# Order of the two products in a block of fp32 matrix products: neighbours in opposite orders, or long and short alternating

## The chip, the core and the metric

The kernel runs on one core of one Trainium2 chip. The metric is the device time of one execution in microseconds (us); of the kernel before, the median of three runs is 771.32 us (771.22 to 771.48). A second kind of number comes from one further execution that was profiled instruction by instruction. Its engines are named as the profile names them: PE is the matrix engine, PEld its loading of stationary weights, DVE the vector engine, ACT the activation engine, POOL the general one, SP the one that issues most of the transfers.

## What is computed

Two decoder layers on 256 tokens of width 1024, all in float32 at the interface. The first mixes tokens with a short gated convolution, the second with dilated attention (8 heads, 3 dilation groups). Each is followed by a squared-ReLU MLP (1024 to 4096 to 1024) and a gated embedding, and a norm ends it all:

```python
h = x
for i in range(DEPTH):                      # DEPTH = 2
    hn = rmsnorm(h, norm_mix[i])
    if kind == 0:
        mixed = short_conv_mixer(hn, sc_w_in[j], sc_w_conv[j], sc_w_out[j])
    elif kind == 1:
        mixed = dilated_attention_mixer(hn, positions, attn_w_qkv[j], attn_w_o[j])
...
    h = h + mixed
    h = h + squared_relu_mlp(rmsnorm(h, norm_mlp[i]), mlp_w_up[i], mlp_w_down[i])
    ple_gate = jax.nn.sigmoid(rmsnorm(h, norm_ple[i]) @ ple_w_gate[i])
    h = h + ple_gate * (p[i].astype(h.dtype) @ ple_w_proj[i])
return rmsnorm(h, norm_final)
```

Almost all of the work is in the matrix products with the weights: every weight is read once from memory and used for 256 tokens.

## The kernel before

**A product in parts.** To keep float32 accuracy on the faster reduced format, each weight tile and each activation tile is held as a sum of two numbers, a high part (`whi`, `x[0]`) and a low part (`wlo`, `x[1]`). A product is then three: high by high, high by low, low by high. The function `block` (L379 to L411) issues them for one weight tile of 128 by 128, and there are three kinds of block.

- Kind "w" (wide): the weight is stationary. The two activation parts lie side by side in memory (`x[2]`), so that one matmul with `whi` and 512 columns makes two of the three products, into the two halves of a PSUM bank, and one matmul with `wlo` and 256 columns makes the third, into the bank's first half. The halves are added later by `sums` (L419). This is the kind of the up and down projections of the MLP, of queries and keys, and of most of the convolution's input, the output projections too. Below, the 256-column product is called the short one and the 512-column product the long one.
- Kind "n" (narrow): the weight is stationary too, but all three products have 256 columns.
- Kind "t" (turned): the activation is stationary and the weight streams, 384 columns for values ("v"), 512 or 256 in the last stage.

**The order of the work.** A plan written out by hand (`make_plan`, with `mlp_plan`, `gate_plan`, `last_plan`) lists blocks and, between them, steps such as evacuations of a bank (`up_out`, `down_out`, `qk_out`), statistics (`stat`, `spread`) and the attention's scores. The last loop of `tile_trunk` walks through it in order. Wide blocks come in pairs: for each row tile k of the weights one block for half 0 and one for half 1 (`for i in (0, 1)`), each half with a bank of its own (the name of the accumulator ends in i).

**The order within a wide block.** The line that the change replaces (L396) turns the two products of a block round when it belongs to half 1:

```python
products = ((dst[:, 0, :], wlo, x[0][:, k % 2, :]), (flat(dst), whi, flat(x[2][:, k % 2, :, :])))
...
products = products[::-1] if half and (key != "qkv" or col[1] or not col[2]) else products
```

So along a run of wide blocks the matmuls are short, long, long, short, short, long, long, short and so on. The exception is the bracket: the queries and keys of dilation group 0 (`col[1]` is the group) of every head but the first (`col[2]` is the head). There no block is turned round and the matmuls are short, long, short, long. These 16 blocks of a head stand right behind the values ("v") of the head before. The matmuls themselves are issued at L404, whatever their kind.

**Attention.** For each head from 1 to 7 the plan has the wide blocks of group 0 (16 blocks), then `scores` of the head before (from head 2 on; it issues matmuls of the values step at L736 and L746 and of the scores at L692 and L700), then groups 1 and 2 (32 blocks), with `turn` and its transposes (L726), then the values of the head (16 blocks of kind "t").

**The weights' way.** The weights come in slabs of up to 8 tiles (`load_to`, a transfer of up to 512 KB); ACT copies a slab to its high part (L368) and DVE subtracts it for the low part (L307, a helper). `weights` (L372) asks for slabs up to 5 ahead of the one in use, and there are 6 buffers for the split slabs and 5 for the raw ones.

Of the kernel before, what the change touches and what calls it, by code (L numbers as in the profile page):

```python
# [18 lines left out]
NK = D // P  # L19
NP = NK // 2  # L20
FF = 4 * D
# [210 lines left out]
def width(key):  # L232
    return {"v": GROUPS, "gate1": 4, "proj1": 4}.get(key, 1)
# [32 lines left out]
def tile_trunk(ctx: ExitStack, tc: tile.TileContext, plan, slabs, ap, out):  # L266
# [17 lines left out]
    def pair(name, tag="pair", dtype=F32R):  # L284

        if tag == "pair":
            t = apool.tile([P, 2, 2, S], dtype, tag=tag, bufs=PAIR_BUFS, name=name)
        else:
            t = cpool.tile([P, 2, 2, S], dtype, tag=tag, bufs=1, name=name)
        return t[:, :, 0, :], t[:, :, 1, :], t  # L290

    def bank(name):
        return psum.tile([P, 2, S], F32, tag="ps", name=name)
# [9 lines left out]
    def flat(t):  # L303
        return t.rearrange("p i s -> p (i s)")
# [16 lines left out]
    for op in plan:  # L321
        if op[0] != "do":
            key = ((*op[4], op[5]), 0) if op[0] == "w" else (op[4], op[5] if op[0] == "n" else 0)
            left[key] = left.get(key, 0) + 1
    rstd, rows, cur, mask, by_token = {}, {}, {}, {}, {}

    def gain(n, k):
        return gains[:, n * NK + k : n * NK + k + 1]
# [2 lines left out]
    offsets, n = [], 0  # L331
# [40 lines left out]
    def weights(item):  # L372
        si, at = place[item]
        split_to(si + min(LOOK, 1 + si // 3))
        hi, lo = parts[si]
        n = width(item[0]) * P
        return hi[:, at : at + n], lo[:, at : at + n]

    def block(kind, key, k, col, name, half, operand, m=0, cuts=1):  # L379
        name = (*name, half) if kind == "w" else name  # L380
        if name not in opened:
            acc[name] = bank("acc_" + "_".join(map(str, name)))
        left[name, half if kind == "n" else 0] -= 1
        whi, wlo = weights((key, k, col))
        x = state[operand][k // 2]
        if kind == "n":
            dst = acc[name][:, half, :]
            products = ((dst, wlo, x[0][:, k % 2, :]), (dst, whi, x[1][:, k % 2, :]), (dst, whi, x[0][:, k % 2, :]))

            products = (products[2], products[0], products[1]) if key == "proj0" else products  # L390
        elif kind == "w":

            dst = acc[name]
            products = ((dst[:, 0, :], wlo, x[0][:, k % 2, :]), (flat(dst), whi, flat(x[2][:, k % 2, :, :])))

            products = products[::-1] if half and (key != "qkv" or col[1] or not col[2]) else products  # L396
        else:
            n = width(key) * P // cuts
            whi, wlo = (t[:, m * n : (m + 1) * n] for t in (whi, wlo))
            dst = flat(acc[name])[:, :n]  # L400
            xhi, xlo = (t[:, k % 2, half * P : (half + 1) * P] for t in x[:2])
            products = ((dst, xhi, whi), (dst, xhi, wlo), (dst, xlo, whi))
        for n, (to, a, b) in enumerate(products):
            nc.tensor.matmul(  # L404
                to,
                a,
                b,
                start=n == 0 and name not in opened,
                stop=n == len(products) - 1 and left[name, half if kind == "n" else 0] == 0,
                skip_group_check=True,  # L410
            )  # L411
            opened.add(name)
# [269 lines left out]

    def scores(head):

        weights = cur["pr", head] = pair(f"sm{head}", dtype=F32)[2]
        ps = [psum.tile([P, 512], F32, tag="ps", name=f"sc{head}_{b}") for b in (0, 1)]
        rest = values(head - 1) if head else None
        for b in (0, 1):
            own = slice(b * P, (b + 1) * P)
            hi, lo, _ = state["qk"][head]  # L690
            for n, (q, k) in enumerate(((hi, hi), (hi, lo), (lo, hi))):
                nc.tensor.matmul(ps[b][:, :S], q[:, 0, own], k[:, 1, :], start=n == 0, stop=n == 2)  # L692
        if rest:
            rest()
        for b in (0, 1):
            for g in (1, 2):
                t = cur["qk", head, g]
                for r in (0, 1):
                    of, at = slice(b * P + r * 64, b * P + (r + 1) * 64), S + (g - 1 ^ r) * 64
                    nc.tensor.matmul(  # L700
                        ps[b][r * 64 : (r + 1) * 64, at : at + 64], t[:, 0, of], t[:, 1, of], start=True, stop=True
                    )
        for b in (0, 1):
            sm, p = flat(weights[:, b])[:, : S + P], ps[b][:, : S + P]
            stats = [spool.tile([P, 1], F32, tag=f"st{n}_{b}", name=f"st{n}_{head}_{b}") for n in range(2)]

            nc.vector.tensor_tensor_reduce(
                out=sm, in0=p, in1=mask[b], op0=ALU.add, op1=ALU.min, scale=-SCALE, scalar=-NEG, accum_out=stats[0]
            )
            nc.scalar.activation(sm, sm, AF.Exp, bias=stats[0], scale=-1.0, accum_out=stats[1])  # L710
            nc.vector.reciprocal(stats[1], stats[1])
            nc.scalar.activation(sm, sm, AF.Copy, scale=stats[1])
# [16 lines left out]
    def values(head):  # L729
        ps = bank(f"o{head}")  # L730
        v0, v12 = cur.pop(("v", head))
        hi, lo, _ = state["pT"].pop(head)
        for kb in (0, 1):
            vhi, vlo = v0[:, kb, :P], v0[:, kb, P:]
            for n, (a, b) in enumerate(((vhi, hi), (vhi, lo), (vlo, hi))):
                nc.tensor.matmul(  # L736
                    ps[:, 0, :], a, b[:, kb, :], start=kb == 0 and n == 0, stop=False, skip_group_check=True
                )

        def rest():  # L740
            t = cur.pop(("pT12", head))
            for n in range(4):
                q, b, r = slice(n * 64, (n + 1) * 64), n // 2, n % 2
                for m in (0, 1):
                    to = slice(m * 64, (m + 1) * 64)
                    nc.tensor.matmul(  # L746
                        ps[to, 0, q],
                        v12[:, b, r * P + m * 64 : r * P + (m + 1) * 64],
                        t[:, b, r * 64 : (r + 1) * 64],
                        start=False,  # L750
                        stop=n == 3,
                        skip_group_check=True,
                    )
            if head % 2 == 0:
                state["y"][head // 2] = pair(f"y{head // 2}")
            hi, lo = (t[:, head % 2, :] for t in state["y"][head // 2][:2])
            nc.scalar.activation(hi, ps[:, 0, :], AF.Copy)
            nc.vector.tensor_tensor(lo, ps[:, 0, :], f32(hi), ALU.subtract)

        return rest  # L760
# [76 lines left out]
    def last_scale(b, c):  # L837
# [13 lines left out]
        begin=begin, p_in=p_in, x_in=x_in, add_up=add_up, squares=squares, proj_out=proj_out, stat=stat, stat_rows=stat_rows, conv=conv, mix_out=mix_out, up_out=up_out,  # L851
        down_out=down_out, gate_out=gate_out, rope=rope, masks=masks_load, qk_out=qk_out, qk_split=qk_split, v_out=v_out,
        scores=scores, turn=turn, spread=spread, last_values=lambda: values(HEADS - 1)(),
        last_load=last_load, turn_h=turn_h, last_gate=last_gate, last_out=last_out, last_rms=last_rms, last_scale=last_scale,
    )
    for op in plan:
        if op[0] != "do":
            block(*op)
        elif op[1] in URGENT:
            with tc.high_priority(offset=HURRY):  # L860
                steps[op[1]](*op[2:])
        else:
            steps[op[1]](*op[2:])
# [89 lines left out]
```

## Time and profile before

| what | value |
|---|---|
| median of 3 runs | 771.32 us (771.22 to 771.48) |
| the profiled execution, its own time | 771.19 us |
| its span, first to last instruction | 769.4 us |
| mean granted clock of the matrix engine | 0.998 |
| instructions | 12415, of them 4716 matmuls |
| busy: DVE, ACT, POOL | 598.6, 488.7, 8.9 us |
| read from memory | 138.97 MB, 182 GB/s over the span |

A matmul's end is modelled in this profile and neighbours overlap in it, so what a matmul costs in a dense stream isn't its duration (a short one is shown with about 0.28 us, a long one with about 0.40 us) but the distance from its start to the next one's start. The chain of work that ended last gives stretches of the stream by line and accumulator, each with its length and its number of matmuls. The timeline gives the starts; there a row with "x2" merges two neighbours of one form, and its time is that of the first. In rows of groups, "acc_u<-x,whi" is a matmul that writes the accumulator of "u" from an activation tile x and a high weight.

### The profile page before, as it was taken

To read this page: it belongs to the slowest core of one execution; us is meant where nothing else is said; L and a number is where in the kernel's file an instruction comes from. 1 tells how busy PE (TensorE), PEld (TensorE's weight loads), DVE (VectorE), ACT (ScalarE), POOL (GpSimd) and SP (SyncE) were. 2 spreads that over 40 slices of the span, in tenths; PEclk is the share of its full clock that TensorE was granted. 3 is DMA by queue.
4 is the path that set the end of the run, shared out by engine and by line. 5 is a ranking of instruction groups with operands and counts; after the bars stand their busy time and mean duration, and the time that the engine had idled before them with its cause. 6 is when DMAs were issued, how large, how long until landed. Compare 5 with 4: busy or idle time off the path is not lost.

```text
span 769.4 us, 12415 instructions
## 1 busy us (share of the span) xinstructions
PE 761.2 (99%) x4716; PEld 680.2 (88%) x4716; DVE 598.6 (78%) x967; ACT 488.7 (64%) x796; POOL 8.9 (1%) x22
## 2 busy tenths in 40 slices
PE   9999999999999999999999999999999999999996
PEld 9988888888888899989989989989988888888885
DVE  6898789898566668898988978977899887655564
ACT  7765566666444446688887778777666555444453
POOL 0000000000000000000000000000000000000002
PEclk9999999999999999999999999999999999999999
DMA  8855555556555554554555456456465555555521
GB/s 311 312 190 192 195 191 169 190 190 197 188 190 191 192 191 139 191 187 152 169 171 197 152 162 200 147 160 219 138 192 188 193 191 191 187 188 189 184 90 56
DMA packets 42539, 140.83 MB, mean 183 GB/s; under 512 B 4848, under 2 KB 6384, under 8 KB 42480
## 3 DMA queue, kind: packets, MB, share of 16 engines
q1 hardware_dynamic: 41904, 139.39, 54.3%
q8 instruction: 37, 0.61, 0.3%
q10 hardware_dynamic: 576, 0.66, 0.3%
q14 instruction: 22, 0.18, 0.1%
HBM read 138.97 MB, written 1.05 MB: 182 GB/s over the span
## 4 chain that ended last, share of the span: by engine, by line
PE 97%; issue 1%; DMA 1%; DVE 0%; POOL 0%; SPq 0%; POOLq 0%; ACT 0%; DVEq 0%
PE acc_u L404 23%; PE acc_d L404 23%; PE acc_qk L404 18%; PE acc_v L404 9%; PE acc_o L404 6%; PE acc_g L404 5%; PE acc_B L404 3%; PE acc_C L404 3%; PE acc_X L404 3%; PE acc_p L404 1%; PE o L736 1%; PE sc L692 1%; PE o L746 1%; DMA raw<-in_w 1%; PE sc L700 1%
## 5 line engine op out<-in xcount | busy, mean ns | idle before, releaser
L307 DVE TENSOR_TENSOR wlo<-raw,whi 128x1024 fp32r<-128x1024 f32 (+2 forms) x277 | 319.2, 1155 | 126.4 <-ACT whi L368 123.9
L368 ACT ACTIVATE whi<-raw 128x1024 fp32r<-128x1024 f32 (+2 forms) x277 | 277.9, 1007 | 166.2 <-PE acc_d L404 77.1
L404 PE MATMUL acc_u<-x,whi 128*128 128x512 f32 x512 | 160.8, 396 | 0.0
L404 PE MATMUL acc_d<-u,whi 128*128 128x512 f32 x512 | 160.8, 395 | 0.0
L404 PE MATMUL acc_qk<-x,whi 128*128 128x512 f32 x384 | 124.6, 395 | 0.0
L404 PEld LDWEIGHTS acc_d<-u,wlo 128*128 128x128 f32 x512 | 96.2, 188 | 22.7
L404 PEld LDWEIGHTS acc_u<-x,wlo 128*128 128x128 f32 x512 | 96.0, 188 | 22.5
L404 PE MATMUL acc_u<-x,wlo 128*128 128x256 f32 x512 | 101.3, 278 | 0.0
L404 PE MATMUL acc_d<-u,wlo 128*128 128x256 f32 x512 | 100.9, 278 | 0.0
L404 PE MATMUL acc_qk<-x,wlo 128*128 128x256 f32 x384 | 86.9, 280 | 0.0
L404 PEld LDWEIGHTS acc_qk<-x,wlo 128*128 128x128 f32 x384 | 72.1, 188 | 12.1
L404 PEld LDWEIGHTS acc_u<-x,whi 128*128 128x128 f32 x512 | 78.0, 189 | 0.2
L404 PEld LDWEIGHTS acc_d<-u,whi 128*128 128x128 f32 x512 | 77.9, 189 | 0.0
L404 PE MATMUL acc_v<-whi,x 128*128 128x384 f32 x256 | 67.2, 337 | 0.0
L404 PEld LDWEIGHTS acc_qk<-x,whi 128*128 128x128 f32 x384 | 62.5, 188 | 4.6
L404 PEld LDWEIGHTS acc_v<-whi,x 128*128 128x128 f32 x256 | 46.5, 188 | 0.1
L404 PE MATMUL acc_v<-wlo,x 128*128 128x384 f32 x128 | 42.9, 335 | 0.0
L423 ACT ACTIVATE r<-acc_u 128x256 f32<-128x256 f32 x64 | 24.1, 378 | 27.8 <-PE acc_u L404 27.5
L404 PE MATMUL acc_o<-y,whi 128*128 128x512 f32 (+1 forms) x144 | 41.0, 370 | 0.0
L655 ACT ACTIVATE rot<-qk 16x512 f32<-16x512 f32 x48 | 30.3, 632 | 9.9 <-DVE qk L424 9.2
L424 DVE TENSOR_TENSOR r<-acc_u,r 128x256 f32<-128x256 f32 x64 | 26.5, 419 | 3.5 <-ACT r L423 3.0
L404 PEld LDWEIGHTS acc_o<-y,wlo 128*128 128x128 f32 x128 | 24.0, 188 | 5.0
(175 smaller groups left out, 976.4 us busy)
## 6 DMA issues: line engine op xcount, KB each, us to landing
raw<-in_w SPq DMA_DIRECT2D x230, 512.0 KB, 3.6
raw<-in_w SPq DMA_DIRECT2D x32, 384.0 KB, 3.4
raw<-in_w SPq DMA_DIRECT2D x10, 256.0 KB, 4.9
h<-in_xT SPq DMA_DIRECT2D x4, 256.0 KB, 5.0
gain<-in_gain SPq DMA_DIRECT2D x2, 256.0 KB, 4.6
out<-htg SPq DMA_DIRECT2D x2, 256.0 KB, 2.1
mask<-in_mask SPq DMA_DIRECT2D x2, 192.0 KB, 3.4
raw<-in_w ACTq DMA_DIRECT2D x2, 128.0 KB, 3.7
```

Source lines behind the costliest of these rows:

```text
L307: nc.vector.tensor_tensor(out, a, f32(b), ALU.subtract)
L368: nc.scalar.activation(hi[:, :width], t[:, :width], AF.Copy)
L404: nc.tensor.matmul(to, a, b, start=n == 0 and name not in opened, stop=n == len(products) - 1 and left[name, half if kind == "n" else 0] == 0,
L423: nc.scalar.activation(t[:, i, :], p[:, 1, :], AF.Copy)
L424: nc.vector.tensor_tensor(t[:, i, :], p[:, 0, :], t[:, i, :], ALU.add)
L655: nc.scalar.activation(r[dst : dst + 16], p[src : src + 16], AF.Copy)
L692: nc.tensor.matmul(ps[b][:, :S], q[:, 0, own], k[:, 1, :], start=n == 0, stop=n == 2)
L700: nc.tensor.matmul(ps[b][r * 64 : (r + 1) * 64, at : at + 64], t[:, 0, of], t[:, 1, of], start=True, stop=True)
L736: nc.tensor.matmul(ps[:, 0, :], a, b[:, kb, :], start=kb == 0 and n == 0, stop=False, skip_group_check=True)
L746: nc.tensor.matmul(ps[to, 0, q], v12[:, b, r * P + m * 64 : r * P + (m + 1) * 64], t[:, b, r * 64 : (r + 1) * 64], start=False, stop=n == ...
```

## The change

It replaces the rule that turns a block round by its half with one that counts wide blocks in a run. A counter is set to 0 by a narrow block and by `scores`, and to a large even number by a turned block; each wide block reads it and adds 1. The block is turned round (long first) when the count is odd or over 1.

```diff
@@ tile_trunk
-    rstd, rows, cur, mask, by_token = {}, {}, {}, {}, {}
+    rstd, rows, cur, mask, by_token, wide_run = {}, {}, {}, {}, {}, {}
@@ block
         x = state[operand][k // 2]
+        if kind != "w":
+
+            wide_run["n"] = 0 if kind == "n" else NK * FF
         if kind == "n":
...
-            products = products[::-1] if half and (key != "qkv" or col[1] or not col[2]) else products
+
+            done = wide_run.get("n", 0)
+            wide_run["n"] = done + 1
+            products = products[::-1] if done % 2 or done > 1 else products
@@ scores
+        wide_run["n"] = 0
         weights = cur["pr", head] = pair(f"sm{head}", dtype=F32)[2]
```

A run behind narrow blocks or behind `scores` therefore begins short, long, long, short, and goes on long, short, long, short to its end. A run behind values is long, short from its first block on. No instruction is added or taken away, no tile, transfer or buffer is changed; the numbers of matmuls of each form stay the same, and each bank receives the same products.

## Prediction

> **What bounds the kernel.** I read the page first, for the engine that fills the span and for the chain that ended last.
>
> ```profile
> span 769.4 us, 12415 instructions
> PE 761.2 (99%) x4716; PEld 680.2 (88%) x4716; DVE 598.6 (78%) x967; ACT 488.7 (64%) x796; POOL 8.9 (1%) x22
> PEclk9999999999999999999999999999999999999999
> PE 97%; issue 1%; DMA 1%; DVE 0%; POOL 0%; SPq 0%; POOLq 0%; ACT 0%; DVEq 0%
> ```
>
> The matrix engine is the kernel: 99% of the span busy, 97% of the chain, at full clock in every slice. A busy share says little where neighbouring matmuls overlap, so the waits come next, for the matrix engine alone and then for all.
>
> ```profile
> PE warm L531 <- DVE power L527: 1.0, 1, 1.0
> ACT whi L368 <- PE acc_d L404: 77.1, 46, 2.0
> ACT whi L368 <- issue: 44.1, 30, 2.4
> ```
>
> The matrix engine waited once, at the start. It is the other way round: ACT, which makes the high parts of the weights, waited 77.1 us for the matrix engine to free buffers. So the supply runs ahead, and what a matmul costs is its distance to the next one. The change adds no matmul and removes none; it can only alter these distances. So the question is whether the distance depends on the order of long and short. The chain in order of time gives stretches: start, length, accumulator, number of matmuls.
>
> ```profile
> 68.47 5.57 PE acc_X L404 x32
> 102.08 44.59 PE acc_u L404 x256
> 191.50 89.17 PE acc_d L404 x512
> 643.54 89.17 PE acc_d L404 x512
> 414.00 5.55 PE acc_qk L404 x32
> 470.39 5.55 PE acc_qk L404 x32
> 498.58 5.55 PE acc_qk L404 x32
> ```
>
> The first four are in the paired order (short, long, long, short). A block is two matmuls, so 512 matmuls are 256 blocks: 89.17 / 256 = 348.3 ns a block, the same in both layers; 44.59 / 128 = 348.4; 5.57 / 16 = 348.1. The last three are the exception in the old rule: group 0 of a head, 16 blocks short, long, short, long. They take 5.55 us where 16 paired blocks take 5.57. The old kernel has therefore made the experiment already, in seven heads, and the trace has both orders on the same tiles and the same kind of weights. The difference is close to the view's rounding, so I go to the starts in the timeline: first the alternating stretch of one head, then paired blocks of the same head.
>
> ```profile
> 470.23 0.28 PE L404 MATMUL acc_qk<-x,wlo 128*128 128x256 f32 x1
> 470.34 0.40 PE L404 MATMUL acc_qk<-x,whi 128*128 128x512 f32 x1
> 470.58 0.28 PE L404 MATMUL acc_qk<-x,wlo 128*128 128x256 f32 x1
> ...
> 475.20 0.40 PE L404 MATMUL acc_qk<-x,whi 128*128 128x512 f32 x1
> 475.43 0.28 PE L404 MATMUL acc_qk<-x,wlo 128*128 128x256 f32 x1
> ```
>
> ```profile
> 481.85 0.40 PE L404 MATMUL acc_qk<-x,wlo 128*128 128x256 f32 x2
> 482.08 0.63 PE L404 MATMUL acc_qk<-x,whi 128*128 128x512 f32 x2
> 482.55 0.39 PE L404 MATMUL acc_qk<-x,wlo 128*128 128x256 f32 x2
> 482.78 0.62 PE L404 MATMUL acc_qk<-x,whi 128*128 128x512 f32 x2
> 483.24 0.40 PE L404 MATMUL acc_qk<-x,wlo 128*128 128x256 f32 x2
> ```
>
> Alternating, from the first short product to the sixteenth: 475.43 - 470.23 = 5.20 us in 15 blocks, 346.7 ns a block. Paired, in rows that merge two neighbours: one pair of blocks takes 482.55 - 481.85 = 0.70 us, the next 483.24 - 482.55 = 0.69. Read to the nanosecond, the 254 undisturbed pairs within the two acc_d stretches quoted above fall in two modes that take strict turns, 704 ns (128 pairs) and 689 to 690 ns (126 pairs), mean 696.7. The undisturbed alternating pairs of group 0 are all near 693.3. That is 3.4 ns a pair, 1.7 ns a block, in favour of alternation; the rows above give the same (348.3 - 346.7 = 1.6).
>
> **The change part by part.** How many blocks change their order? The wide blocks are the ones with a 512-column product from a high weight:
>
> ```profile
> L404 PE MATMUL acc_u<-x,whi 128*128 128x512 f32 x512 | 160.8, 396 | 0.0
> L404 PE MATMUL acc_d<-u,whi 128*128 128x512 f32 x512 | 160.8, 395 | 0.0
> L404 PE MATMUL acc_qk<-x,whi 128*128 128x512 f32 x384 | 124.6, 395 | 0.0
> L404 PE MATMUL acc_o<-y,whi 128*128 128x512 f32 x112 | 35.1, 395 | 0.0
> L404 PE MATMUL acc_X<-x,whi 128*128 128x512 f32 x64 | 20.1, 395 | 0.0
> L404 PE MATMUL acc_C<-x,whi 128*128 128x512 f32 x48 | 15.1, 395 | 0.0
> L404 PE MATMUL acc_B<-x,whi 128*128 128x512 f32 x32 | 10.1, 395 | 0.0
> ```
>
> They sum to 1664 blocks. Of these 7 heads x 16 = 112 alternate already, so 1552 blocks, 776 pairs, stand in the paired order. Going through the plan with the new counter, a run begins anew in 15 places and keeps its first pair there: 4 in the convolution's input (behind narrow blocks of B), 1 at its output projection, 7 behind scores (heads 2 to 7 and the attention's output projection), and 3 behind other narrow blocks: at the first queries, within the attention's output projection and at the second up projection. That leaves 761 pairs that go from paired to alternating.
>
> *Main term.* 761 x (696.7 - 693.3) ns = 2.6 us; with the coarser rows 2 x 761 x (348.3 - 346.7) = 2.4 us. I take 2.5 us off. The starts are rounded to 10 ns, so the 5.20 us may be off by 0.01, 0.7 ns a block, 1.0 us in all: 1.4 to 3.5 us.
>
> *What the trace does not show.* The alternating blocks of before begin with the short product; in the new order all blocks but the first of a run begin with the long one. As a string of sizes it is the same string, but the step from long to short now stays in one bank and the step from short to long goes to the other half's bank. Before, long to short within one bank occurs in each block of half 1, and such a pair costs 689 to 704. So the unseen order is bounded by those two modes: if all pairs were the cheap one, 761 x (696.7 - 689.5) = 5.5 us less; all dear, 761 x (704 - 696.7) = 5.6 us more. I take the alternating value, since dear and cheap pairs contain exactly the same steps on the same banks and differ only in turn; the sizes decide, not the banks.
>
> *The mirror image in group 0.* 112 blocks go from short first to long first behind values: the same steps but for one in each head, at nought, between the same two bounds for 56 pairs, 0.4 us either way.
>
> *What hides the rest.* No DMA, evacuation or split moves in the plan. Within a block the long product wants the high part, which ACT makes before DVE makes the low part, so long first asks for the earlier of the two; nothing new is late. If the supply could not follow, the gain would stop there; but 2.5 us in 769 asks 0.3% more of ACT at 64% and DVE at 78%. The last wide blocks of an accumulator end with a long and a short product for half 1 before and after, so the evacuations follow the stream by the same distance.
>
> *Sum.* The profiled execution took 771.19 us (span 769.4 and 1.8 around it); 771.19 - 2.5 = 768.7. The median shown is 0.13 above that execution, so 768.8 for the median.
>
> **The rivals.** *The order is worth nothing: 771.3.* A product's distance would be its own and follow it wherever it stands. For it speaks a run of short products alone (narrow blocks of the gate):
>
> ```profile
> 291.64 12.95 PE acc_g L404 x108
> ```
>
> 12.95 / 108 = 119.9 ns each; a long one then costs 348.3 - 119.9 = 228.4, and the paired order shows just such a sum. Against it stand the seven alternating stretches, which are cheaper than that sum. If their saving came from the place behind values rather than from the order, this rival holds. The Trainium skill, in "TensorE: Matmul & The Clock Gate", section "Back-to-back issue gap", gives a rule of this kind: the isolated gap is the columns over 2.4 GHz and 2.5 ns more, whatever the neighbours. By that rule a block would take 109.2 + 215.8 = 325.0 ns in either order (an estimate from that page), so the change would bring nothing; the trace agrees neither with the size, 348.3, nor with the indifference to order.
>
> *Slower: 776.9.* The place is the step from long to short in one bank. If that step is what makes a dear pair dear, every block has it now where every second block had it, and all 761 pairs cost 704 ns: 5.6 us more. It decides from the point where a new pair averages over 696.7 ns. For it: no alternating stretch of before has this step. Against it: the cheap pairs have it too.
>
> *A larger gain: 765.8.* The new pairs settle in the cheap mode. Nothing in the trace of before prefers it.
>
> **How the numbers follow.** My forecast has 0.74: 768.8, its own range 767.8 to 769.9 by the rounding above. No effect has 0.13, slower 0.06, the larger gain 0.07. A change of 0.2% is 1.5 us, about what a measurement of this kernel can tell from none. The forecast and the larger gain are faster by more than that but for a small part, 0.02, where the gain is nearer its lower end: 0.79 faster, 0.15 the same, 0.06 slower. The forecast alone holds less than 8 in 10, so the range reaches to no effect, 771.5, and at the lower end to the forecast's 767.8.
>
> **What would show it.** In the profile after, the chain's acc_d stretches should read 88.75 us (256 x 346.7) in place of 89.17, and X, C and B of the convolution 5.55 each in place of 5.57; the timeline of acc_d should no longer merge neighbours and should show starts 0.23 and 0.12 apart. The qk stretches of group 0 stay at 5.55. Stretches at 89.2 mean no effect; at 90.1 (128 x 704) the slower rival; at 88.2 the larger gain. I am wrong in kind if the stretches shrink and the span doesn't: then a new wait of the matrix engine must appear.

## The result, and the profile after

The changed kernel takes 774.3 us in the median (773.8 to 777.73, 7 runs), the kernel before 771.28 us (771.07 to 771.6, 7 runs). The ratio is 1.0051 with a 95% interval of 1.0033 to 1.0069: slower by 3.0 us where 2.5 us less was forecast. Five of the seven times lie between 773.80 and 775.13, two at 777.57 and 777.73; I come back to that gap.

The page of the profiled execution (774.19 us) answers to the lines shown of before, with the same number of matmuls, at full clock but for the last slice:

```profile
span 772.4 us, 12419 instructions
PE 764.2 (99%) x4716; PEld 683.5 (88%) x4716; DVE 598.9 (78%) x967; ACT 488.5 (63%) x796; POOL 8.9 (1%) x22
PEclk9999999999999999999999999999999999999998
```

The four instructions more are waits for semaphores in the matrix engine's queue (44 by the records, 40 before), so the change does add instructions, if no work. They don't make the difference: `short_first` below has 39, and its layer 0 is as dear.

The view of waits has the same single one for the matrix engine as before:

```profile
PE warm L537 <- DVE power L533: 1.0, 1, 1.0
```

So the 3 us lie inside the stream. The chain in order of time (start, length, accumulator, number of matmuls; a block is two of them) says where:

```profile
68.46 5.55 PE acc_X L410 x32
79.76 22.60 PE acc_o L410 x128
102.35 45.24 PE acc_u L410 x256
147.82 45.23 PE acc_u L410 x256
193.05 90.45 PE acc_d L410 x512
...
360.55 5.65 PE acc_qk L410 x32
...
388.79 5.55 PE acc_qk L410 x32
...
453.52 11.50 PE acc_qk L410 x64
...
557.72 44.64 PE acc_u L410 x256
602.59 44.37 PE acc_u L410 x256
646.96 88.75 PE acc_d L410 x512
```

The reader is to compare the two stretches of acc_d. It is the same product with the same order, tiles of the same size and the same number of blocks, once per layer. In layer 1 it takes 88.75 us, 346.7 ns a block, exactly what was forecast. In layer 0 it takes 90.45 us, 353.3 ns a block; before, both took 89.17. The convolution's stretches are at the forecast too (5.55 / 16 = 346.7). By stretch, in us:

| stretch | before | after | difference |
|---|---|---|---|
| convolution, six stretches of 16 blocks | 5.57 each | 5.55 each | -0.1 |
| first output projection | 22.30 | 22.60 | +0.3 |
| up0, two halves | 44.59 + 44.60 | 45.24 + 45.23 | +1.3 |
| down0 | 89.17 | 90.45 | +1.3 |
| first queries and keys (76 matmuls) | 13.24 | 13.42 | +0.2 |
| groups 1 and 2 of heads 3 to 7 | 11.36 each | 11.50 each | +0.7 |
| up1, two halves | 44.76 + 44.60 | 44.64 + 44.37 | -0.35 |
| down1 | 89.17 | 88.75 | -0.4 |

They sum to +2.9 us of the 3.0 by which the span grew. Group 0 of heads 3 to 7, behind values, stays at 5.55 us, but that of head 2, behind values too, went from 5.56 to 5.65: 353.1 ns a block.

The timeline shows what a dear block looks like. First layer 0's acc_d, then layer 1's:

```profile
200.19 0.28 PE L410 MATMUL acc_d<-u,wlo 128*128 128x256 f32 x1
...
200.54 0.28 PE L410 MATMUL acc_d<-u,wlo 128*128 128x256 f32 x1
...
200.89 0.28 PE L410 MATMUL acc_d<-u,wlo 128*128 128x256 f32 x1
...
201.25 0.28 PE L410 MATMUL acc_d<-u,wlo 128*128 128x256 f32 x1
```

```profile
699.72 0.28 PE L410 MATMUL acc_d<-u,wlo 128*128 128x256 f32 x1
...
700.07 0.28 PE L410 MATMUL acc_d<-u,wlo 128*128 128x256 f32 x1
...
700.76 0.28 PE L410 MATMUL acc_d<-u,wlo 128*128 128x256 f32 x1
```

Read the starts of the short products. Above they are 0.35, 0.35 and 0.36 us apart, below three steps are 700.76 - 699.72 = 1.04 us, even steps of 0.347. To the nanosecond the records of the dear stretch repeat every three blocks: 113 from the short to the long product and 233 to the next short one, then 117 and 241, then 120 and 236, together 1060 ns. In the cheap stretch each block is near 117 and 230. Nothing waits in either by the profile; a dear block has 6.7 ns more between its starts.

### The profile page after: what moved, and what is told of

Read it like the earlier page. It is cut to its first block, busy times and chain, and to the rows that moved or that the text cites. A ratio compares the mean times of both kernels' runs of the same rounds, so it can differ in the third digit from the quotient of the medians.

```text
span 772.4 us, 12419 instructions
## 1 busy us (share of the span) xinstructions
PE 764.2 (99%) x4716; PEld 683.5 (88%) x4716; DVE 598.9 (78%) x967; ACT 488.5 (63%) x796; POOL 8.9 (1%) x22
## 4 chain that ended last, share of the span: by engine, by line
PE 98%; issue 1%; DVE 0%; POOL 0%; POOLq 0%; DVEq 0%
PE acc_u L410 23%; PE acc_d L410 23%; PE acc_qk L410 18%; PE acc_v L410 9%; PE acc_o L410 6%; PE acc_g L410 5%; PE acc_B L410 3%; PE acc_C L410 3%; PE acc_X L410 3%; PE acc_p L410 1%; PE sc L699 1%; PE o L743 1%; PE o L753 1%; PE sc L707 1%; PE tp L733 0%
## 5 line engine op out<-in xcount | busy, mean ns | idle before, releaser
L410 PE MATMUL acc_u<-x,whi 128*128 128x512 f32 x512 | 179.4, 395 | 0.0
L410 PE MATMUL acc_d<-u,whi 128*128 128x512 f32 x512 | 179.3, 395 | 0.0
L410 PE MATMUL acc_u<-x,wlo 128*128 128x256 f32 x512 | 143.6, 280 | 0.0
L410 PE MATMUL acc_d<-u,wlo 128*128 128x256 f32 x512 | 143.6, 280 | 0.0
L410 PE MATMUL acc_qk<-x,whi 128*128 128x512 f32 x384 | 134.6, 396 | 0.0
L410 PEld LDWEIGHTS acc_d<-u,whi 128*128 128x128 f32 x512 | 96.0, 187 | 22.5
L410 PEld LDWEIGHTS acc_u<-x,whi 128*128 128x128 f32 x512 | 95.9, 187 | 22.5 <-DVE x L454 0.2
L410 PE MATMUL acc_qk<-x,wlo 128*128 128x256 f32 x384 | 108.4, 282 | 0.0
L410 PE MATMUL acc_o<-y,wlo 128*128 128x256 f32 x128 | 35.8, 283 | 0.0
L410 PEld LDWEIGHTS acc_o<-y,whi 128*128 128x128 f32 x144 | 25.7, 189 | 4.7
```

What stands on the lines that cost most here:

```text
L410: nc.tensor.matmul(to, a, b, start=n == 0 and name not in opened, stop=n == len(products) - 1 and left[name, half if kind == "n" else 0] == 0,
```

## The experiments

Three theories were on the table. **Locking**: an alternating stream has a cheap and a dear steady state, and how it is entered decides which one it falls into. **Place**: the tiles and banks of layer 0 make alternation dear there. **Opening**: the opposite first pair of a run, which the change puts in front, does it.

**Other openings.** Three kernels differ from the changed one only in this line, and `again` differs in nothing:

```diff
-products = products[::-1] if done % 2 or done > 1 else products
+products = products                                              # short_first
+products = products[::-1]                                        # long_first
+products = products[::-1] if done % 2 or done > 3 else products  # two_pairs
```

`again`: 

> The changed kernel once more, unaltered. Seen so far: in the alternating order the convolution's stretches and those of layer 1's MLP cost 346.7 ns a block, those of the first output projection and layer 0's MLP 353.3, nothing between. Locking theory (an alternating string has a cheap and a dear steady state, and the way it is entered decides which one it falls into): stretches are again at 346.7 or 353.3; layer 0's, entered without a wait on data, falls the same way again, down0 at 90.4 us; layer 1's, entered behind a wait whose length varies, may fall either way, which would explain single runs 3.5 us longer (512 blocks x 6.7 ns). Place theory (the tiles and banks of layer 0's MLP make it dear): down0 90.4 and down1 88.75 in every execution. Opening theory (the opposite first pair of a run causes the dear state): as the place theory in this run.

`short_first`: 

> All wide blocks short first, no opposite first pair anywhere: the alternation that group 0 had before, everywhere. Opening theory: without the opposite pair every stretch is cheap, down0 88.75 us, total near 768.8. Place theory: layer 0's MLP stays dear, down0 90.4, total near 774. Locking theory: each stretch is at 346.7 or 353.3 and nothing between; which one can't be said beforehand, but it may differ from the changed kernel's in either direction; total between 768.7 and about 779 (all dear).

`long_first`: 

> All wide blocks long first, no opposite first pair anywhere. Opening theory: every stretch cheap, down0 88.75 us, total near 768.8. Place theory: down0 90.4, total near 774. Locking theory: each stretch 346.7 or 353.3 according to its entry; a run that starts long behind values is cheap as in the changed kernel (its 5.55 us stretches of group 0), a run that starts long behind narrow blocks has not been seen; total between 768.7 and about 779.

`two_pairs`: 

> As the changed kernel, but a run behind narrow blocks or scores begins with two opposite pairs before it alternates. In the paired order dear and cheap pairs (704, 689 ns) take turns, so the alternation now begins one turn later. Locking theory: the entry of the first output projection is another one, and layer 0's MLP may fall into the cheap state: down0 88.75 us, total near 771. Place theory: down0 90.4. Opening theory: an opposite pair stands there still, so dear, 90.4.

Measured: again 774.64 us (one run); short_first 773.91 us, ratio 1.0032 (1.0020 to 1.0044); long_first 777.38 us, ratio 1.0076 (1.0061 to 1.0091); two_pairs 778.3 us (one run). In ns a block, undisturbed:

| stretch | again | short_first | long_first | two_pairs |
|---|---|---|---|---|
| convolution, later stretches | 346.7 | 346.7 | 353.1 to 353.8 | 353.1 to 353.8 |
| layer 0's MLP | 353.3 | 353.3 | 353.3 | 353.3 |
| layer 1's MLP, second half of up1 and down1 | 346.7 | 346.7 | 353.3 | 353.3 |

The opening theory falls: in short_first and long_first, with no opposite pair in front, layer 0 is as dear as in the changed kernel. The bare place theory loses the convolution and layer 1, which are cheap or dear on the same tiles. But layer 0's MLP was dear four times out of four, so place was not yet out for it. My guess for two_pairs, cheap in layer 0, was wrong.

Layer 1 of short_first holds a surprise. The matmuls of up1 don't all stand in the plan's order there, and at one place two long products meet:

```profile
563.15 0.52 PE L410 MATMUL acc_u<-x,wlo 128*128 128x256 f32 x3
563.51 0.63 PE L410 MATMUL acc_u<-x,whi 128*128 128x512 f32 x2
```

By the records up1's blocks cost 353.3 ns up to this place and 346.7 from 564.7 us on. So it wasn't the entry that made layer 1 cheap in this kernel; what two such products do is tried below.

**Dummy matmuls in layer 0.** `kicks` puts dummies into the changed kernel's layer 0, in a bank that nobody reads (the lines of the plan that call `kick` are left out):

```diff
...
+    def kick(turned):
+        ps = flat(bank("kick"))
+        if turned:
+            nc.tensor.matmul(ps[:, :384], ones_r, flat(state["u"][0][2][:, 0, :, :])[:, :384], start=True, stop=True)
+        else:
+            for n in range(4):
+                nc.tensor.matmul(ps[:, 2 * n : 2 * n + 2], ones, ones[:, :2], start=True, stop=True)
...
```

> The changed kernel with dummy matmuls added to layer 0's MLP, into a bank that nobody reads: four fp32 matmuls of 2 columns (as a statistics step issues) behind up0's blocks of j=3 and j=10, one matmul of 384 columns behind down0's j=0 and j=2. In the changed kernel these 512 blocks cost 353.3 ns throughout. Locking theory: an interruption can throw the stream from one state to the other, so between two of these marks the blocks change to 346.7 at least once, with tiles, banks and order of the wide blocks unaltered; if all of the blocks behind the first mark became cheap, some 448 x 6.7 ns = 3.0 us less, against about 1.3 us for the dummies. Place theory (layer 0's tiles or banks): all blocks stay at 353.3 and the total grows by about 1.3 us. Supply theory (the weights come too late for alternation there): as place, or less dear by the pauses.

Measured: 775.16 us (one run). The chain between the dummies:

```profile
102.32 22.62 PE acc_u L414 x128
125.73 22.30 PE acc_u L414 x128
148.26 16.64 PE acc_u L414 x96
165.69 28.36 PE acc_u L414 x160
194.06 22.62 PE acc_d L414 x128
216.85 44.38 PE acc_d L414 x256
261.41 22.20 PE acc_d L414 x128
```

Before the first dummy 64 blocks take 22.62 us, 353.4 ns each. The four matmuls of 2 columns, eight rows in the trace, take 0.79 us. Behind them blocks settle at 346.7 (16.64 / 48), behind the second such dummy they are dear again (22.62 for 64 blocks of acc_d), and a single 384-column matmul at 216.5 us turns the rest of down0 cheap: 44.38 / 128 and 22.20 / 64 are 346.7 and 346.9. So the same weights in the same order have two prices within one run. The supply theory doesn't fit: it lets a pause help at most, and behind the second pause the stream became dear. Of place one form is left, since each dummy takes one of the pool's eight banks, so that the accumulators behind it may stand in other banks than in the changed kernel; the seams below have no dummy and settle that. Of the 448 blocks behind the first dummy some 304 were cheap and not all: a dummy can also throw a cheap stream into the dear state.

**Another entry.** `entries` puts one 384-column dummy in front of the first output projection and of the first queries, and starts long first there, as behind values.

> The changed kernel with one dummy matmul of 384 columns in front of the first wide block of the first output projection and of the first queries and keys, both of which follow a run of narrow blocks, and with the order behind values there (long, short from the first block). Locking theory: a 384-column matmul in front makes the entry that of values, behind which all stretches seen are cheap: sc_out, up0 and down0 at 346.7 (down0 88.75 us), the first qk stretch too; total 774.2 - 576 x 6.7 ns - 38 x 6.7 ns + 0.4 = 770.5. If one long matmul doesn't undo what a run of narrow blocks has set up, 353.3 and 774.6. Place theory: 353.3 and 774.6.

Measured: 775.57 us (one run), and not as I had it: the first output projection and the first half of up0 stayed dear. The premise was wrong already, for head 2's group 0 is dear behind values (5.65 us in the changed kernel).

```profile
102.75 45.22 PE acc_u L412 x256
148.22 44.38 PE acc_u L412 x256
192.59 88.75 PE acc_d L412 x512
...
646.63 90.45 PE acc_d L412 x512
```

Then the two matmuls of the statistics step within up0 (at 147.8 us) turned the stream cheap, and down0 took 88.75 us where it took 90.45 in the changed kernel, on the same code (though perhaps in other banks, as in kicks). Layer 1, whose code is the changed kernel's too, was dear this time: 90.45 where it was 88.75. Its MLP cost 3.4 us more than in the profile of the changed kernel. That is the gap between the two groups among that kernel's seven times (777.6 against 774.2); that those two executions had layer 1 dear would fit, but they were not profiled.

The start of up1 suggests how little it takes. Here a matmul seems to wait for data: by the records the first long product of the changed kernel starts 0.28 us after the short one, where the dense stream has 0.12, and 0.06 us after DVE has ended a tile of x (at 557.78 us). The view of waits doesn't list it, for the rows of the matmuls overlap. First the changed kernel, then entries:

```profile
557.55 0.28 PE L410 MATMUL acc_u<-x,wlo 128*128 128x256 f32 x1
557.83 0.72 PE L410 MATMUL acc_u<-x,whi 128*128 128x512 f32 x2
558.39 0.28 PE L410 MATMUL acc_u<-x,wlo 128*128 128x256 f32 x1
```

```profile
555.50 0.28 PE L412 MATMUL acc_u<-x,wlo 128*128 128x256 f32 x1
555.78 0.74 PE L412 MATMUL acc_u<-x,whi 128*128 128x512 f32 x2
556.36 0.28 PE L412 MATMUL acc_u<-x,wlo 128*128 128x256 f32 x1
```

From the first to the third row it is 0.84 us in the one and 0.86 in the other. By the records it is 842 and 861 ns. The first stream is cheap from there on, the second dear. In three more executions with the same order here it was 842 ns (again), cheap, 847 (kicks), dear, and 860 (flips41), dear. That the start decides is not shown; it goes with the state five times out of five.

**Seams.** `flips41` lets the order in the first output projection and layer 0's MLP turn over every 41 blocks:

```diff
...
+if key in ("sc_out", "up0", "down0"):
+    at = wide_run["at"] = wide_run.get("at", -1) + 1
+    turned = at // 41 % 2
...
```

> The changed kernel, but in the first output projection and layer 0's MLP (576 blocks) the order turns over every 41 blocks: 41 blocks short first, 41 long first, and so on, so that two long ones, then two short ones, meet at the seams. Locking theory: single seams are enough to change the state, and stretches between seams are at 346.7 or 353.3, some of each. If a seam never changes it, all 353.3. Place theory: all 353.3. Theory of the bank (long to short in one bank is the dear step): long-first stretches 353.3, short-first stretches 346.7, in strict turns.

Measured: 775.61 us (one run; layer 1 was dear, 90.45). In layer 0 the stretches between seams are at 353.3 or 346.7, some of each, and neither order owns a state: the second stretch (long first) is cheap, the third (short first) too, the fourth (long first) dear, the fifth (short first) dear. The theory of the bank, my rival "slower" in the prediction, falls with that. The first seam, where two long products meet (the row with x2), ended the dear state; behind it the records settle at 117 and 230 ns:

```profile
93.50 0.28 PE L414 MATMUL acc_o<-y,wlo 128*128 128x256 f32 x1
93.62 0.64 PE L414 MATMUL acc_o<-y,whi 128*128 128x512 f32 x2
94.10 0.28 PE L414 MATMUL acc_o<-y,wlo 128*128 128x256 f32 x1
```

Read to the nanosecond, the other seams say more. At seven seams two long products meet, and each of these changed the state: three from dear to cheap, all behind a block of 117 to 118 and 240 to 241 ns, and four from cheap to dear. At six two short ones meet, and none of these changed it. (The last seam has too few blocks behind it to tell.)

**A mixed order, then one seam.** `mixed` alternates only where it had been cheap with short first:

```diff
+products = products[::-1] if half and key not in ("sc_in", "up1", "down1") and (key != "qkv" or col[1] or not col[2]) else products
```

> Alternation, short first, where it was cheap with short first everywhere (convolution's input, group 0 of heads 1 to 7, layer 1's MLP); the old paired order in the output projections, layer 0's MLP and the other queries and keys. Paired stretches should cost 348.3 everywhere under all theories. Locking theory: layer 1's MLP is entered as before or by another way now, so 346.7 or 353.3; if cheap, total 771.3 - 0.1 (convolution) - 0.9 (512 blocks x 1.7 ns) = 770.3, if dear 773.8. Place theory: 770.3 for sure.

Measured: 770.4 us (769.97 to 770.63, 10 runs), ratio to before 0.9987 (0.9977 to 0.9997); down0, paired, 89.17, down1 88.75. `seam17` adds the alternation of layer 0 with one seam, at the turn at which the seam of flips41 had helped:

```diff
...
+if key in ("sc_out", "up0", "down0"):
+    at = wide_run["at"] = wide_run.get("at", -1) + 1
+    turned = at >= 17
...
```

> The mixed order (paired in the later output projection and the other queries and keys, short first alternating in the convolution, group 0 and layer 1's MLP), but the first output projection and layer 0's MLP, paired there, now alternate too, with one seam: 17 blocks short first, all later ones long first. In the kernel with a seam every 41 blocks the first seam took the dear stream to the cheap state, behind a block whose distances were 117 and 241; the dear state repeats every 3 blocks and 17 is 41 less 24, so the seam meets the same turn. Locking theory: 17 blocks at 353.3, the other 559 of the stretch at 346.7 through both products of the MLP: down0 88.75 us in place of 89.17, total 770.4 + 0.1 - 0.9 = 769.6. If the state depends on more than this turn: 353.3 behind the seam, total 773.3.

Measured: 769.38 us (769.13 to 769.96, 9 runs), ratio 0.9976 (0.9966 to 0.9986), the fastest kernel of this study. The chain:

```profile
101.96 44.37 PE acc_u L414 x256
146.57 44.37 PE acc_u L414 x256
190.94 88.75 PE acc_d L414 x512
```

**Does the turn decide?** `seam16` and `seam18` have 16 and 18 in place of 17.

> As the kernel with the seam behind 17 blocks, with the seam one block earlier. The dear state repeats every 3 blocks, so the seam now meets another of its three turns. If the turn decides: down0 may stay at 90.45 us, total near 773; if any seam of two long products cures the dear state, down0 88.75 and total near 769.4.

> The same with the seam one block later, at the third turn. If the turn decides, at least one of these two kernels stays dear (down0 90.45 us, total near 773); if any such seam cures, both are near 769.4.

Measured: 773.24 and 773.53 us (one run each). Both stay dear through layer 0, while down1 is cheap in all three. First seam16, then seam18:

```profile
193.10 90.45 PE acc_d L414 x512
646.02 88.75 PE acc_d L414 x512
```

```profile
193.41 90.45 PE acc_d L414 x512
646.30 88.75 PE acc_d L414 x512
```

By the records, the last block ahead of the seam was the one of 117 and 241 ns in seam17, the one of 113 and 233 in seam16, the one of 120 and 236 in seam18. One block earlier or later costs 3.9 to 4.2 us. Place falls here in every form: the three kernels have the same tiles, no dummy, the same sequence of accumulators and in down0 the same order, and down0 takes 88.75 us in one and 90.45 in two.

**Is the short product too short?** `short384` widens it from 256 to 384 columns, which adds the product of the low parts for half of the tokens.

```diff
-products = ((dst[:, 0, :], wlo, x[0][:, k % 2, :]), ...
+products = ((flat(dst)[:, :384], wlo, flat(x[2][:, k % 2, :, :])[:, :384]), ...
```

> The changed kernel with its short product widened from 256 to 384 columns (it adds the product of the low parts for 128 tokens; the products that were there stay). A product alone costs 120 (256 columns), 173.3 (384) and 226.7 ns (512), so a block would be 400.0 ns without interaction. Load theory (the dear state comes from a short product that is no longer than a weight load, so that a late load is never caught up): 384 columns leave room, every stretch is 400.0 and the two states are gone; down0 102.4 us. Locking theory in its general form (any alternating string has two states, whatever the lengths): some stretches above 400 by 6 to 7 ns, the stretch from the first output projection to down0 among them, 104.1.

Measured: 876.0 us (one run). Two levels again, 406.7 and 413.3 ns a block (128 and 256 blocks in these rows), and none at 400.0, the sum of 226.7 and of the 173 to 174 ns that a product of 384 columns takes in the stretches of values:

```profile
114.89 52.05 PE acc_u L410 x256
167.18 52.90 PE acc_u L410 x256
220.07 105.81 PE acc_d L410 x512
```

The load theory in that form falls; the two states don't need a short product of 256 columns. My figure for the locking theory was off too: the upper level lies 13.3 above the sum and not 6 to 7, and the lower one isn't the sum, as it is with 256 columns. The switch from the lower to the upper level stands at the statistics step between the halves of up0 here.

## Why the prediction was wrong

The range, 767.8 to 771.5 us, missed 774.3, and the sign was wrong.

- *What bounds the kernel*: right. The view of waits lists the same single wait of the matrix engine before and after; the distances in its stream moved.
- *The count* of 761 pairs: right. By the records two long products follow each other in 776 places before and in 16 after, the 15 of the working and one that is not in the plan's order.
- *The main term*, 761 x 3.4 ns: here it failed. The step took the price of alternation from seven stretches of 16 blocks behind values and gave it to all 1522 blocks. Those stretches were one state of two, and not even that entry is safe: head 2's, one of the seven, is dear in the changed kernel. Where the stream was in that state the price was right to the rounding (346.7 ns in the convolution and layer 1); elsewhere it was 353.3, 5.0 above the paired order. Over 780 blocks fell there: 576 from the first output projection to down0, 48 in the first queries and keys, 160 in groups 1 and 2 of heads 3 to 7, and a few shorter stretches, head 2's group 0 among them, which the term for the mirror image had at nought.
- *What the trace does not show*: I bounded the unseen order by the two modes of the pairs, 5.5 us less to 5.6 more. The measured 3.0 more lies inside, and the dear state of 353.3 lies just outside, above the dear pair's 352. I then took the alternating value because "the sizes decide, not the banks". The banks indeed don't decide. But nor do the sizes alone: the same string of sizes has two prices.
- *The rival of no effect* worked with a long product of 228.4 ns, got by taking 119.9 from a paired block. That figure already held an interaction. Long products alone stand in before's last stage:

```profile
733.71 0.61 PE L404 MATMUL acc_g<-whi,x 128*128 128x512 f32 x2
734.16 0.39 PE L404 MATMUL acc_g<-wlo,x 128*128 128x512 f32 x1
734.39 0.61 PE L404 MATMUL acc_g<-whi,x 128*128 128x512 f32 x2
734.84 0.39 PE L404 MATMUL acc_g<-wlo,x 128*128 128x512 f32 x1
735.07 0.61 PE L404 MATMUL acc_g<-whi,x 128*128 128x512 f32 x2
```

Six products from 733.71 to 735.07, in 1.36 us, are 226.7 ns each, and 226.7 + 119.9 = 346.6. The cheap state is thus the bare sum of both products; the paired order costs 1.7 ns a block over it and the dear state 6.7. I might have seen that alternation had reached a floor in the seven stretches, and asked what keeps a stream off it.
- *The rival "slower"* had the right sign, by luck: it put 5.6 us, and not 3.0, on the step from long to short in one bank, and flips41 shows both orders in both states.
- *The rule from the Trainium skill*: "TensorE: Matmul & The Clock Gate", section "Back-to-back issue gap", gives the gap by the columns for an isolated matmul, and says that in a stream of weight loads and matmuls both set the spacing. The prediction took the gap to hold whatever the neighbours, which the section doesn't say. Its 325.0 ns a block (an estimate from that page) is met by no stretch here: the same matmuls took 346.7, 348.3 and 353.3.

What stays open is why. The runs show that there are two states, that a stream keeps its state over hundreds of blocks, and what switches it; not which part of the matrix engine holds it. That weight loads play a part was argued only, and their rows can't tell: in down0 and down1 after they are 187 to 192 ns long in both states.

## What to carry to other kernels

When a stream of matmuls is dense, price an order by the sum of its products alone (each from a run of its own kind) and treat anything above as an interaction that may depend on history; a cheaper stretch elsewhere in the trace is one sample of it, however many times the same entry repeats. Before generalizing, find the same order behind several kinds of entry: narrow products, waits, statistics. And after such a change look at each stretch, not at the total: two stretches of the same product at 88.75 and 90.45 us say at once that the order is not the cause by itself. Read the order from the timeline, too, for it isn't the plan's everywhere.

## What the runs showed of the hardware

- A stream of 256- and 512-column products with a new weight tile each has two steady states when they alternate, 346.7 and 353.3 ns a block, and one, 348.3, when equal neighbours are paired, in all paired stretches seen. The paired order costs 1.7 ns but did not depend on its entry.
- The dear state repeats every three blocks. Two long products in a row ended it at one of its three turns and left it at the other two (769.38 against 773.24 and 773.53 us). Where they fell into a cheap stream, in flips41, it was dear behind them, four times out of four.
- Four matmuls of 2 columns, two of 256 or a single one of 384 each switched the state at least once, the first kind either way. They don't always: the two of 256 left layer 0 dear in the changed kernel. Behind a wait for data, starts that differed by 5 to 19 ns went with the one state or the other.
- With 384 columns in place of 256 the two levels were 406.7 and 413.3, both above the bare sum of 400.0.
